# Values channel-major, a last inverse from 16x16 blocks, an early attention output and like tile addresses in a hybrid attention and RWKV-7 layer

## The chip, the cores and the metric

The kernel runs on one core of one Trainium2 chip. The time is the device time of one launch in microseconds (us); for the kernel before it is the median of three runs. A core has TensorE (PE, matrix products; PEld is its weight load), VectorE (DVE), ScalarE (ACT), GpSimd (POOL) and SyncE (SP, whose queue starts the transfers). Each engine works through its own list of instructions in order.

## The reference

One layer of a decoder over 512 positions of width 1024, all in 32-bit floats. What matters here:

```python
ada = (c @ w_ada + b_ada)                      # six rows of 1024: shift, scale and gate, twice
h = rms_norm(x, norm1_w) * (1.0 + sc1) + sh1
att_in, rwkv_in, gate_in = split(h @ w_in)
# attention: 3 groups of (window, dilation), 8 heads of 64 channels, blocks of 128 queries
p = exp(scores - m); den = sum(p)
num = einsum('bnrhqk,bnkrhe->bnqrhe', p, v)    # "values"
out_g = num / den_g; lse_g = m_g + log(den_g)
y_att = sum_g(softmax_g(lse)[..., None] * out_g) @ w_att_out     # "shares" of the groups
# RWKV-7: 16 heads, a 64x64 state each, one step a position
state = state * w_t + (state @ a_t) b_t + v_t k_t
y_rwkv = (group_norm(state @ r_t) + bonus) * g @ w_rwkv_out
x = x + gt1 * ((sigmoid(g_att) * y_att + sigmoid(g_rwkv) * y_rwkv) @ w_o)
x = x + gt2 * (silu(conv(gate)) * conv(val)) @ w_down            # after adaLN(x) @ w_up
out = rms_norm(x, norm_f_w)
```

## The kernel before

Products with weights are made of three products of a high and a low half (`mm`, L148: high by high, high by low, low by high), each 128x128 stationary and 512 columns moving. A weight comes as `raw` by DMA, ACT copies its high half `whi` (L193, L1136) and DVE subtracts the low half `wlo` (L194, L1139). Products of attention and of the recurrence are single 32-bit products. Transposes go through PE with `ident` (`tr`, L151).

**Order.** Up to the end of the recurrence the work is a list of tasks with an engine, a guessed cost in us, the tasks that they need, a priority and the buffers that they take and give (`Plan.add`, `Plan.run`, L47). The plan is run once at build time with those costs, and the order in which tasks start there is the order of the instructions on each engine. What comes after (`rwkv_out`, the mixing with `w_o`, the feed-forward part) is in the order of the code, as the tile scheduler lays it out. PE's order mixes long rows of 512-column products, used as filler, with the short steps that wait for other engines.

**Attention.** Three groups `gi`. For a block `n` of 128 queries and a pair of heads `i`, `scores` (`sc`) go through DVE (`sm`) and ACT (`pr`, exponentials) to PE transposes (`pt`), are copied to `pts`, and `values` gives `po`: here the probabilities `pts` are stationary (128x128) and `v` moves (64 columns), so a row is a query. `out` copies `po` to `o`. Groups 0 and 1 are later combined with the shares (`al` tasks): DVE multiplies `o` by the share (L1017), PE transposes the result (`pa<-ident,o`), ACT copies it to `attT` and a DMA stores it to `att_d`.

**Conditioning.** `w_ada` comes in 512 KB pieces `araw` through two buffers; DVE adds them into `acc` (L347), PE sums `acc` over partitions (`ada`).

**Recurrence.** Eight pairs of heads in four groups `g`; each group has a preparation (`pair`), an `inverse` and a `chain`. The sequence is cut into eight chunks of 64. The inverse of unit triangular 64x64 matrices is made of 32x32 blocks: DVE steps on all blocks at once, two columns a step (L1512, L1514, L1515) and then single ones (L1504, L1505), transposes (L1521, L1526), and two PE rounds `pe` of 32 products each that join the blocks (copies at L1567 and L1569). The chain then goes chunk by chunk: `xy` (state by inputs), `xs` (L1641), solve into `u`, `uv` (L1654), output `xo`, state `mbd` (L1664) with `mp` from POOL (L1646). It starts with a fill of `u` (L1589) and the product `u<-cen,v`.

**Gates and outputs.** Sixteen gate rows of 128 channels (`pg` tasks, `early_gate`) are made as filler, stored to `gate_d` and loaded back (L1825, `early_gates`) once the preparation's buffers are closed (`t0`); `t1` comes after group 0 and 2's tiles are closed too. `att_out` loads `att_d` (L1841), splits it (`ahi` L1843, `alo` L1844) and forms `pa` with `w_att_out`; `pr` is the same for the recurrence with `y`. Then `o` (with `w_o`, weights `wohi`, `wolo`), `u` (w_up, moving `h2hi`, `h2lo`) and `o` again (w_down).

Of the kernel before, what the change touches and what calls it, by code (L numbers as in the profile page):

```python
# [128 lines left out]
class Layer:  # L129
# [72 lines left out]
    def consts(self):  # L202
        nc, ctx, tc = self.nc, self.ctx, self.tc
        self.cp = cp = ctx.enter_context(tc.tile_pool(name="cp", bufs=1))
        self.dr = ctx.enter_context(tc.tile_pool(name="dr", bufs=1, space=DRAM))
        self.ident = cp.tile([P, P], F32, name="ident")
        make_identity(nc, self.ident)
        self.ones = cp.tile([P, 1], F32, name="ones")
        nc.gpsimd.memset(self.ones, 1.0)
        self.mhalf = cp.tile([P, 1], F32, name="mhalf")  # L210
# [9 lines left out]
        self.sel2 = cp.tile([P, 2], F32, name="sel2")  # L220
# [411 lines left out]

    def mask2(self):
# [38 lines left out]
    def attention(self):  # L672
# [4 lines left out]
        o = [ap.tile([P, 4, ATT_W], F32, name="o0"), None]  # L677
# [110 lines left out]
        def attend(gi, hf, order, blocks, width, mask, V, ready, prio):  # L788
# [4 lines left out]
            for n, i, new, end in order:  # L793
# [37 lines left out]
                def values(n=n, i=i, d=d, new=new, end=end):  # L831
                    if new:
                        pos[n] = self.aps.tile([P, 256], F32, tag="po", name=self.n("po"), bufs=2)
                    vs = V(n)
                    for h in range(2):
                        cs = slice(i * P + h * 64, i * P + h * 64 + 64)
                        for j, v in enumerate(vs):
                            self.mm(pos[n][:, cs], d["pts"][:, h, j * P : (j + 1) * P], v[:, cs],
                                    new and h == 0 and j == 0, end and h == 1 and j == len(vs) - 1)

                def out(n=n, i=i, new=new):
                    c0, c1 = (i * P if new else 0), i * P + P
                    if gi and o[1] is None:
                        o[1] = ap.tile([P, 4, ATT_W], F32, tag="o1", name="o1")
                    nc.scalar.copy(o[gi][:, n, hf * 256 + c0 : hf * 256 + c1], pos[n][:, c0:c1])
# [11 lines left out]
                t = pe(0.9 * wd / 256, values, [t], S0, take=("po",) if new else (), give=("pts",), name="po")  # L857
# [110 lines left out]
        for _ in ada:  # L968
            pass

# [23 lines left out]
        scaled = []  # L994
        for gi in range(2):
            a, b = stt[gi], oth[gi]
            mn, ea, eb, dn = [ap.tile([P, 4, 8], F32, name=f"{s}{gi}") for s in ("mn", "ea", "eb", "dn")]

            def diff(a=a, b=b, mn=mn, ea=ea, eb=eb):
                nc.vector.tensor_tensor(mn, a[:, :, 0, :], b[:, :, 0, :], op=ALU.min)  # L1000
                nc.vector.tensor_tensor(ea, mn, a[:, :, 0, :], op=ALU.subtract)
                nc.vector.tensor_tensor(eb, mn, b[:, :, 0, :], op=ALU.subtract)

            def exps(ea=ea, eb=eb):
                nc.scalar.activation(ea, ea, AF.Exp)
                nc.scalar.activation(eb, eb, AF.Exp)
# [12 lines left out]
            t = sca(0.45, exps, [t], name="al")  # L1019
            t = dve(1.2, share, [t], name="al")  # L1020
            scaled += [dve(0.7, lambda n=n, scale=scale: scale(n), [t, *outs[gi]], name="al") for n in range(4)]
        for i in range(4):
            d = {}

            def turn(i=i, d=d):
                d["pa"] = self.aps.tile([P, S], F32, tag="pt", name=self.n("pa"), bufs=2)
                for n in range(4):
                    self.tr(d["pa"][:, n * P : (n + 1) * P], o[0][:, n, i * P : (i + 1) * P], n == 0, False)
                for n in range(4):
                    self.tr(d["pa"][:, n::4], o[1][:, n, i * P : (i + 1) * P], False, n == 3)  # L1030

            def out(d=d):
                d["t"] = self.awl.tile([P, S], F32, tag="attT", name=self.n("attT"), bufs=2)
                nc.scalar.copy(d["t"], d["pa"])
            t = pe(0.95, turn, scaled, take=("pt",), name="pa")
            t = sca(0.6, out, [t], take=("attT",), give=("pt",), name="pa")
# [4 lines left out]
    def rwkv(self, tail):  # L1041
# [17 lines left out]
        def half():  # L1059

            self.half = self.ip.tile([P, 2], F32, name="half")
            nc.vector.tensor_reduce(self.half, self.ident.rearrange("p (q s y) -> p s q y", q=4, s=2), axis=AX.XY,
                                    op=ALU.add)
# [7 lines left out]
        for g in range(4):  # L1071
            for i in range(2):
                self.pair(g, i)
            self.inverse(g)
            self.chain(g)
        for m in range(2 * KD):
            self.early_gate(m)
# [12 lines left out]
        self.att_out(t1)  # L1090
# [480 lines left out]

    def chain(self, g):
# [42 lines left out]
        for c in range(NCH):  # L1615
# [62 lines left out]
            so_ = pe(0.33 if c else 0.0, state_out, [st], C_ + 0.01, take=("xo",), name="xo")  # L1678
# [26 lines left out]
        for i in range(2):  # L1705
# [43 lines left out]
            t = pe(1.05, gate, [t, self.sgs], S_, take=("t",), give=("g2",), name="gg")  # L1749
            gt_ = sca(0.6, gate_out, [t], E_, take=("gg",), give=("t",))  # L1750
# [32 lines left out]
    def norm(self, yts, t, deps, T_):  # L1783
# [9 lines left out]
        def var():  # L1793
            d["var"] = cw.tile([P, 4], F32, tag="var", name=self.n("var"))
            nc.vector.tensor_reduce(d["var"], d["sq"], axis=AX.X, op=ALU.add)

        def scale():
            rs = cw.tile([P, 4], F32, tag="rs", name=self.n("rs"))
# [19 lines left out]
    def gates(self, opened):  # L1818
# [4 lines left out]
        def load(m):  # L1823
            self.p[m] = self.pp2.tile([P, S], F32, name=f"gate{m}", tag=f"gate{m}")
            nc.sync.dma_start(self.p[m], self.gd[m])  # L1825
        for m in range(KD):
            self.pt[m] = self.pl.add("DMA", 0.8, lambda m=m: load(m), [opened, self.gdt[m]], M_, lag=2.0, name="gate in")

    def early_gates(self, pool):
        self.tr_ = [pool.tile([P, S], F32, name=f"gate{m}", tag=f"gate{m}") for m in range(KD, 2 * KD)]  # L1830
# [16 lines left out]
    def open_late(self, pool, lp):  # L1847

        self.lp = lp
        self.ahi, self.alo = [pool.tile([P, 4, S], F32R, name=x, tag=x) for x in ("ahi", "alo")]  # L1850
        self.yhi, self.ylo = [lp.tile([P, KD, S], F32R, name=x, tag=x) for x in ("yhi", "ylo")]

    def att_out(self, opened):

        nc = self.nc
        parts = [self.load_part(lambda k=k: self.att_d[:, k, :], lambda k=k: self.ahi[:, k, :],
                                lambda k=k: self.alo[:, k, :], lambda: self.lp, [opened], 0.01 * k) for k in range(4)]
        for m in range(KD):
            t, d = self.body("pa", self.w_att_out[0][:, m * P : (m + 1) * P], 4, "psb", lambda: self.psb("pa"),
                             lambda k: (self.ahi[:, k, :], self.alo[:, k, :]), deps=[opened], late=parts)  # L1860
# [181 lines left out]
    def ffn_down(self, xp, op, psx):  # L2042
# [30 lines left out]
        for n in range(NT):  # L2073
# [4 lines left out]
            ss, sofar = op.tile([P, 3], F32, name=self.n("ss"), tag="ss2"), None  # L2078
# [36 lines left out]
def hybrid_layer_kernel(ctx, tc, out, *args, dbg=None):  # L2115
# [11 lines left out]
    with ExitStack() as mix:  # L2127
# [7 lines left out]
        def tail():  # L2135
            L.psb = psum(att, "bps", 2, side="right")
            L.pp2 = right.enter_context(pool("pp2", side="right"))

            def more():
                yp = right.enter_context(pool("yp", side="right"))  # L2140
                L.open_late(att.enter_context(pool("attp", side="right")), yp)
            return more
# [3 lines left out]
        L.early_gates(right.enter_context(pool("gtp", side="right")))  # L2146
# [58 lines left out]
```

## Time and profile before

| | |
|---|---|
| Runs | 1233.17, 1234.45, 1236.06 us; median 1234.45 |
| Profiled execution | 1231.72 us, span 1230.0 us, mean granted clock 0.984 |
| PE busy | 1179.3 us, 96% of the span |
| DVE, ACT, POOL busy | 750.2, 542.4, 109.2 us |
| Moved by DMA | 139.41 MB, mean 113 GB/s |

A row of the timeline has the start, the duration, the engine, the line of the kernel, the operation, out<-in, the array shape (rows*columns of the PE array in use), partitions x elements, and a count; in brackets stands the idle time ahead of it and what ended it. Products overlap, so the pace is read from one start to the next, not from the durations. A row of the windows has the stretch, its length, the busy time of each engine with the count of its instructions, the clock that TensorE was granted, the share of DMA time and GB/s. One matmul of a 32-bit product shows twice in the trace (x8 for four).

### The profile page before, as it was taken

The page shows a single profiled execution, that of the slowest core. Times are in us where ns is not written, and L with a number is a line of the kernel's source. Part 1 is how long each engine was busy: PE and PEld are TensorE (multiplying, and loading weights), DVE is VectorE, ACT ScalarE, POOL GpSimd, SP SyncE. Part 2 cuts the span into 40 slices and gives each one's busy share as a digit, 9 for nine tenths or more (in the row PEclk, how much of TensorE's full clock was granted, in tenths as well). Part 3 has the DMA queues.
Part 4 walks back from the last instruction along what each step waited for, and adds up shares of the span by engine and source line. Part 5 has one row for each costly group of instructions (what it writes and reads, how often), then busy time and mean ns, then how long its engine had stood idle before and what let it go on. Part 6 is the DMA issues. An engine that isn't in the chain of part 4 may idle for free.

```text
span 1230.0 us, 18481 instructions
## 1 busy us (share of the span) xinstructions
PE 1179.3 (96%) x7200; PEld 946.1 (77%) x7200; DVE 750.2 (61%) x1266; ACT 542.4 (44%) x1011; POOL 109.2 (9%) x228
## 2 busy tenths in 40 slices
PE   4999999999999999999999599999999999999997
PEld 3788887889778776767786467788888888878886
DVE  5687862431668977846896844764556556652135
ACT  4374521522565474465545443444444444442123
POOL 4000000000000013132103122014000000000001
PEclk9899999999999999999999799999999999999999
DMA  9845872120233342413241525460232323233331
GB/s 316 249 132 166 273 229 66 45 80 18 69 103 94 90 112 74 126 47 98 80 114 43 163 58 178 156 206 18 69 103 86 103 86 102 86 103 103 103 120 68
DMA packets 168902, 139.41 MB, mean 113 GB/s; under 512 B 8849, under 2 KB 150251, under 8 KB 168815
## 3 DMA queue, kind: packets, MB, share of 16 engines
q1 hardware_dynamic: 168671, 137.98, 37.0%
q8 instruction: 56, 0.92, 0.3%
q14 instruction: 31, 0.25, 0.1%
q10 hardware_dynamic: 144, 0.26, 0.1%
HBM read 127.65 MB, written 10.56 MB: 112 GB/s over the span
## 4 chain that ended last, share of the span: by engine, by line
PE 79%; DVE 11%; DMA 6%; ACT 2%; issue 2%; SPq 0%; POOL 0%; POOLq 0%; DVEq 0%; ACTq 0%
PE u L148 22%; PE o L148 13%; PE v L148 7%; PE pg L148 7%; PE qk L148 5%; DMA araw<-in_w_ada_dram 4%; PE k L148 3%; PE r L148 2%; PE pa L148 2%; PE pr L148 2%; PE early L148 2%; PE po L148 2%; PE xy L148 2%; PE pt L151 1%; DVE tt L1514 1%
## 5 line engine op out<-in xcount | busy, mean ns | idle before, releaser
L194 DVE TENSOR_TENSOR wlo<-raw,whi 128x1024 fp32r<-128x1024 f32 x65 | 79.7, 1225 | 146.7 <-ACT whi L193 146.6
L148 PE MATMUL u<-h2lo,whi 128*128 128x512 f32 (+2 forms) x368 | 142.3, 387 | 0.0
L148 PE MATMUL u<-h2hi,whi 128*128 128x512 f32 (+2 forms) x368 | 142.3, 387 | 0.0
L148 PE MATMUL u<-h2hi,wlo 128*128 128x512 f32 (+2 forms) x368 | 142.2, 386 | 0.0
L1136 ACT CAST whi<-raw 128x1024 fp32r<-128x1024 f32 (+2 forms) x73 | 72.5, 994 | 123.7 <-PE qk L148 49.5
L193 ACT CAST whi<-raw 128x1024 fp32r<-128x1024 f32 x65 | 68.2, 1049 | 106.5 <-PE o L148 53.7
L1139 DVE TENSOR_TENSOR wlo<-raw,whi 128x1024 fp32r<-128x1024 f32 (+2 forms) x73 | 83.7, 1149 | 19.1 <-ACT whi L1136 18.8
L148 PEld LDWEIGHTS u<-h2lo,whi 128*128 128x128 f32 x368 | 68.9, 187 | 16.0 <-POOL h2lo L405 0.2
L148 PEld LDWEIGHTS u<-h2hi,wlo 128*128 128x128 f32 x368 | 68.9, 187 | 15.5
L148 PEld LDWEIGHTS u<-h2hi,whi 128*128 128x128 f32 x368 | 68.9, 187 | 15.4
L2028 DVE SCALAR_TENSOR_TENSOR u<-u,cols,u 128x511 f32<-128x511 f32 x88 | 65.7, 747 | 4.3 <-ACT u L2026 2.7
L148 PE MATMUL qk<-hhi,wlo 128*128 128x512 f32 x160 | 64.0, 400 | 0.0
L148 PE MATMUL qk<-hlo,whi 128*128 128x512 f32 x160 | 63.6, 397 | 0.0
L148 PE MATMUL qk<-hhi,whi 128*128 128x512 f32 x160 | 63.5, 397 | 0.0
L148 PE MATMUL o<-whi,fhi 128*128 128x512 f32 x144 | 56.1, 390 | 0.3 <-DVE u L2028 0.3
L148 PE MATMUL o<-wlo,fhi 128*128 128x512 f32 x144 | 56.0, 389 | 0.0
L148 PE MATMUL o<-whi,flo 128*128 128x512 f32 x144 | 56.0, 389 | 0.0
L148 PE MATMUL pg<-hhi,wlo 128*128 128x512 f32 x128 | 51.8, 405 | 0.0
L148 PE MATMUL pg<-hlo,whi 128*128 128x512 f32 x128 | 51.7, 404 | 0.0
L148 PE MATMUL pg<-hhi,whi 128*128 128x512 f32 x128 | 51.7, 404 | 0.0
L810 DVE CUSTOM_DVE_ANT_0 sm<-sc,m 128x256 f32<-128x256 f32 (+1 forms) x64 | 23.9, 404 | 37.6 <-PE sc L148 36.5
L347 DVE SCALAR_TENSOR_TENSOR acc<-araw,cols,acc 128x1024 f32<-128x1024 f32 x28 | 35.8, 1280 | 17.2 <-DMA araw<-in_w_ada_dram 17.1
(414 smaller groups left out, 2778.3 us busy)
## 6 DMA issues: line engine op xcount, KB each, us to landing
raw<-in_w_in_dram SPq DMA_DIRECT2D x62, 512.0 KB
raw<-in_w_up_dram SPq DMA_DIRECT2D x44, 512.0 KB
araw<-in_w_ada_dram SPq DMA_DIRECT2D x32, 512.0 KB
raw<-in_w_down_dram SPq DMA_DIRECT2D x22, 512.0 KB
araw<-in_w_ada_dram SPq DMA_DIRECT2D x32, 256.0 KB
wvraw<-in_w_in_dram SPq DMA_DIRECT2D x20, 256.0 KB
gate_d<-gs SPq DMA_DIRECT2D x16, 256.0 KB
gate<-gate_d SPq DMA_DIRECT2D x16, 256.0 KB
```

Of the source, the lines that this page charges most:

```text
L148: return self.nc.tensor.matmul(out, lhsT, rhs, start=start, stop=stop)
L151: self.nc.tensor.matmul(out, in_, self.ident[: in_.shape[0], : in_.shape[0]], is_transpose=True, start=start, stop=stop,)
L193: self.nc.scalar.copy(hl[0], raw)
L194: (lo_eng or self.nc.vector).tensor_tensor(hl[1], raw, hl[0], op=ALU.subtract)
L347: nc.vector.scalar_tensor_tensor(d["acc"], raw, ck, d["acc"], op0=ALU.mult, op1=ALU.add)
L810: nc.vector.tensor_tensor_reduce(d["sm", h][:, :wd], d["sc"][h][:, :wd], m[:, 256 - wd : 256] if gi == 0 else m[:, :wd], 1.0, 3.0e38, op0= ...
L1136: nc.scalar.copy(d["w"][0], d["raw"])
L1139: nc.vector.tensor_tensor(d["w"][1], d["raw"], d["w"][0], op=ALU.subtract)
L1514: nc.vector.tensor_reduce(t[:, n0:, j - 1 : j + 1], x, axis=AX.X, op=ALU.add)
L2028: nc.vector.scalar_tensor_tensor(u[:, d:], pu[:, : S - d], ch(c), u[:, d:], op0=ALU.mult, op1=ALU.add)
```

## The change

1. `values` has `v` stationary (128x64, one head) and the probabilities moving (128 columns); the two heads of a pair go to the two halves of `po`'s partitions. A row of `po` and `o` is now a channel.
2. The groups' shares are no longer multiplied into `o` ahead of the transposes. The shares (8 heads by 128 queries, four times) are transposed, split into halves in `share`, and spread over the channels by a product with a selector, `pw<-share,heads`; DVE multiplies `o` by `pw` from PSUM and POOL adds the two groups into `attT`. `heads` is filled on POOL.
3. Group 3's inverse is `inverse16`: blocks of 16x16, so six pair steps and three single ones, and two more PE rounds (`half_pe`, 64 products of 32x16 each) ahead of the two old ones; `first` is a fill and a copy on POOL.
4. Gate 7 is made after `t0` straight into its place, with no store or load.
5. `att_out` opens at `t0` instead of `t1` and loads `att_d` in two pieces of 512 KB through the weights' `raw` buffers; its halves `ahi`, `alo` are eight tiles that share room with gates 8 to 15.
6. In a chunk's `state` the products with `uv` come ahead of those with `mbd`, and `state_out` has the priority to follow at once.
7. Small tiles are packed (`ones`, `mhalf`, `sel2`, `half` in `few`; `var` and `rs` in one tile; `sup` narrower), so that the tiles behind them begin at other addresses.

```diff
-        self.ones = cp.tile([P, 1], F32, name="ones")
+        few = cp.tile([P, 8], F32, name="few")
+        self.ones, self.mhalf, self.sel2, self.half = few[:, 0:1], few[:, 1:2], few[:, 2:4], few[:, 4:6]
...
-                    for h in range(2):
-                        cs = slice(i * P + h * 64, i * P + h * 64 + 64)
-                        for j, v in enumerate(vs):
-                            self.mm(pos[n][:, cs], d["pts"][:, h, j * P : (j + 1) * P], v[:, cs],
+                    for j, v in enumerate(vs):
+                        for h in range(2):
+                            c0 = i * P + h * 64
+                            self.mm(pos[n][h * 64 : h * 64 + 64, i * P : i * P + P], v[:, c0 : c0 + 64],
+                                    d["pts"][:, h, j * P : (j + 1) * P], new and j == 0, end and j == len(vs) - 1)
...
-            def scale(n, gi=gi, ea=ea):
-                ov = o[gi][:, n, :].rearrange("p (h e) -> p h e", h=8)
-                nc.vector.tensor_tensor(ov, ov, ea[:, n, :].unsqueeze(2).to_broadcast([P, 8, 64]), op=ALU.mult)
+            def turn(gi=gi, d=d):
+                d["ps"] = self.aps.tile([P, S], F32, tag="pt", name=self.n("pe"), bufs=2)
+                for n in range(4):
+                    self.tr(d["ps"][:8, n * P : (n + 1) * P], shares[gi][1][:, n, :], n == 0, n == 3)
...
+                self.mm(d["w", gi], self.heads[:, i * P : (i + 1) * P], self.share[gi], True, True)
+            def scale(gi, i=i, d=d):
+                nc.vector.tensor_tensor(o[gi][:, i, :], o[gi][:, i, :], d["w", gi], op=ALU.mult)
-                nc.scalar.copy(d["t"], d["pa"])
+                nc.gpsimd.tensor_tensor(d["t"], o[0][:, i, :], o[1][:, i, :].rearrange("p (r j) -> p j r", r=4), op=ALU.add)
...
-            self.inverse(g)
+            (self.inverse16 if g in (3,) else self.inverse)(g)
             self.chain(g)
+        self.late = range(7, KD)
...
-        self.att_out(t1)
+        self.att_out(t0)
...
+        for j in range(14, 2, -2):
+            t = dve(0.55 + 2 * (16 - j) ** 2 / 480, lambda j=j: two(j), [t], name=f"inv{g}")
+        for j in range(2, -1, -1):
+            t = dve(0.37 + (16 - j) ** 2 / 480, lambda j=j: step(j), [t], name=f"inv{g}")
+        t = [dve(0.27, wide0, [t], E_), sca(0.42, wide1, [t], E_)]
+        tc = dve(1.1, rows, t, E_)
+        t = dve(0.72, rows11, [tc], E_)
+        for j in range(2):
+            t = pl.add("PE", 2.6, lambda j=j: half_pe(j), [t, ey], 0.5, take=() if j else ("t",), name="pe")
+            tc = t = sca(0.42, lambda j=j: half_out(j), [t], 0.5, name="pe")
+        t11 = dve(0.72, rows11, [tc], 0.5)
...
+                for i, h, cs, ci in ih:
+                    self.mm(xy[X[i], cs], gt(i, h, R[i], X[i]), s["uv"][R[i], ci], h == 0, c == 0 and h == 1)
                 for i in range(2 if c else 0):
-                    self.mm(xy[X[i], :P], prs[i]["ar"][:, c, X[i]], mbd(i), True, False)
-                for i, h, cs, ci in ih:
-                    self.mm(xy[X[i], cs], gt(i, h, R[i], X[i]), s["uv"][R[i], ci], c == 0 and h == 0, h == 1)
+                    self.mm(xy[X[i], :P], prs[i]["ar"][:, c, X[i]], mbd(i), False, True)
...
+            if m in self.late:
+                t, d = self.body("gate", self.gate_w(m), KD, "mm", lambda: self.mmp("pg"), self.hT)
+                self.pt[m] = self.pl.add("ACT", 0.7, lambda m=m, d=d: here(m, d), [t, opened], E_, give=("mm",))
...
+            d["t"] = self.wp.tile([P, D], F32, tag="raw", name=self.n("raw"), bufs=2).rearrange("p (k s) -> p k s", k=2)
+            nc.sync.dma_start(d["t"], self.att_d[:, 2 * q : 2 * q + 2, :])
```

The order of instructions at three places. First PE around a unit of values in group 0, in the kernel before (`qk` is the projection for the next queries and keys, used as filler):

```order
L148 MATMUL qk_1656<-hlo,whi_1582 128x512
L148 MATMUL qk_1656<-hhi,wlo_1583 128x512
L148 MATMUL po_1667<-v_1263,pts_1654 128x64 x4
L148 MATMUL qk_1656<-hhi,whi_1582 128x512
L148 MATMUL qk_1656<-hlo,whi_1582 128x512
```

and in the changed kernel:

```order
L148 MATMUL qk_1515<-hhi,whi_1416 128x512
L148 MATMUL qk_1515<-hlo,whi_1416 128x512
L148 MATMUL po_1652<-pts_1642,v_1276 64x128 x4
L148 MATMUL qk_1515<-hhi,wlo_1417 128x512
L148 MATMUL qk_1661<-hhi,whi_1508 128x512
L148 MATMUL qk_1661<-hlo,whi_1508 128x512
```

The unit has the same count of products, with the operands swapped, and it still stands between 512-column products. Second, PE at the end of group 2's chain, before (`t` are group 2's output transposes, `pe` the two rounds that end group 3's inverse, `u_6943` opens group 3's chain):

```order
L151 MATMUL t_6824<-ident,yt_6603 128x128
L151 MATMUL t_6824<-ident,yt_6734 128x128
L151 MATMUL t_6840<-ident,yt_6317 128x128
L151 MATMUL t_6840<-ident,yt_6472 128x128
L151 MATMUL t_6840<-ident,yt_6603 128x128
L151 MATMUL t_6840<-ident,yt_6734 128x128
L148 MATMUL pe_6856<-lt_6496,gt_5851 32x32 x32
L148 MATMUL pe_6856<-tt_6527,lt_6496 32x32 x32
L148 MATMUL u_6943<-cen,v_5833 64x128
```

and in the changed kernel, from the last product of chunk 5 to chunk 6's solve (`pe_6720` with 32x16 are the half rounds):

```order
L148 MATMUL xo_6684<-uv_6583,gt_5222 64x64 x4
L148 MATMUL pe_6720<-lr_6416,gt_5881 32x16 x64
L148 MATMUL xy_6803<-uv_6715,gt_5222 64x64 x4
L148 MATMUL xy_6803<-mbd_84,ar_4931 64x128
L148 MATMUL xy_6803<-mbd_85,ar_5554 64x128
L148 MATMUL xo_6816<-mbd_84,ar_4931 64x128
L148 MATMUL xo_6816<-mbd_85,ar_5554 64x128
L148 MATMUL pe_6720<-lt_6417,lr_6416 32x16 x64
L148 MATMUL u_6246<-xs_6886,gt_5222 64x64 x4
L148 MATMUL pa_6896<-a_6564,whi_6791 128x512
L148 MATMUL pa_6896<-a_6568,whi_6791 128x512
L148 MATMUL pa_6896<-a_6564,wlo_6792 128x512
```

The half rounds stand inside group 2's chain, the first between `xo` of one chunk and `xy` of the next, and the `pa` products come in there; before, the rounds stood behind the whole chain. Third, DVE in group 3's inverse, before (the last pair steps and the first single one; `mbd` is group 2's state):

```order
L1664 SCALAR_TENSOR_TENSOR mbd_86<-u_6232,pc_4931,mp_6686 128x128
L1664 SCALAR_TENSOR_TENSOR mbd_87<-u_6232,pc_5483,mp_6686 128x128
L1512 TENSOR_TENSOR tt_6527<-tt_6527,lt_6496 128x676
L1514 TENSOR_REDUCE tt_6527<-tt_6527 128x13x2
L1515 SCALAR_TENSOR_TENSOR tt_6527<-tt_6527,sup_6537 128x13
L1512 TENSOR_TENSOR tt_6527<-tt_6527,lt_6496 128x784
L1514 TENSOR_REDUCE tt_6527<-tt_6527 128x14x2
L1515 SCALAR_TENSOR_TENSOR tt_6527<-tt_6527,sup_6537 128x14
L1504 TENSOR_TENSOR tt_6527<-tt_6527,lt_6496 128x450
L1505 TENSOR_REDUCE tt_6527<-tt_6527 128x15
```

and in the changed kernel (the last pair step and the single ones; `a_6568` is a low half of the attention input):

```order
L1689 TENSOR_TENSOR lr_6416<-lt_6417 128x288
L1691 TENSOR_REDUCE lt_6417<-lr_6416 128x12x2
L1692 SCALAR_TENSOR_TENSOR lt_6417<-lt_6417,sup_6500 128x12
L2003 TENSOR_REDUCE var_6612<-sq_6600 128x4
L1682 TENSOR_TENSOR lr_6416<-lt_6417 128x182
L1683 TENSOR_REDUCE lt_6417<-lr_6416 128x13
L1682 TENSOR_TENSOR lr_6416<-lt_6417 128x210
L1683 TENSOR_REDUCE lt_6417<-lr_6416 128x14
L2085 TENSOR_TENSOR a_6568<-raw_6572,a_6564 128x512
L1682 TENSOR_TENSOR lr_6416<-lt_6417 128x240
L1683 TENSOR_REDUCE lt_6417<-lr_6416 128x15
L1870 SCALAR_TENSOR_TENSOR mbd_84<-u_6246,pc_4847,mp_6595 128x128
```

Steps are shorter and fewer between two states of the chain, and the splits of `att_out` now stand among them.

More of the change, by code (lines that the diff above doesn't have):

```diff
@@ L631, in masks, with share_rows @@
                 pattern=[[-1, P]], channel_multiplier=1)
+    def share_rows(self):
+        nc = self.nc
+        self.heads = self.awl.tile([P, 2, S], F32R, tag="qk12", name="heads", bufs=1)[:40, 0, :]
+        t = self.awl.tile([P, 2, S], F32R, tag="qk02", name="share", bufs=1)[:40]
+        self.share = [t[:, gi, :] for gi in range(2)]
+        one = lambda r, c: self.ident[r, c : c + 8].unsqueeze(2).to_broadcast([r.stop - r.start, 8, 64])
+        h = self.heads.rearrange("p (h e) -> p h e", e=64)
+        for r, c in ((slice(0, 32), 0), (slice(32, 40), 32)):
+            nc.gpsimd.tensor_copy(h[r], one(r, c))
+        for x in self.share:
+            nc.gpsimd.tensor_copy(x[:32].rearrange("p (h e) -> p h e", e=64), one(slice(0, 32), 64))
     def mask2(self):
@@ L856, in attend @@
                 t = (dve if i else sca)(0.68 if wd == 256 else 0.42, turned, [t], E0, take=("pts",), give=("pt",), name="pts")
-                t = pe(0.9 * wd / 256, values, [t], S0, take=("po",) if new else (), give=("pts",), name="po")
+                t = pe(0.1 + 0.45 * wd / 256, values, [t], S0, take=("po",) if new else (), give=("pts",), name="po")
                 last[i].append(t)
@@ L969, in attention @@
             pass
+        heads = pl.add("POOL", 3.0, self.share_rows, sc, E_, take=("qk02", "qk12"), name="heads")
         def pre():
@@ L1037, in attention @@
+            t = pl.add("POOL", 1.2, out, ts, E_, take=("attT",), name="pa")
             pl.add("DMA", 0.8, lambda i=i, d=d: nc.sync.dma_start(self.att_d[:, i, :], d["t"]), [t], W_, lag=2.0,
@@ L1073, in rwkv @@
                 self.pair(g, i)
[L1074 removed]
+            (self.inverse16 if g in (3,) else self.inverse)(g)
             self.chain(g)
+        self.late = range(7, KD)
         for m in range(2 * KD):
[L1077 removed]
+            if m not in self.late:
+                self.early_gate(m)
         def close_pre():
```

223 lines of the change are left out of this document (184 added, 39 removed).

## The prediction

> **What bounds the kernel now.** I read the page's busy times first, then the span cut into stretches, then the timeline inside each stretch where TensorE (PE) is not full.
>
> ```profile
> span 1230.0 us, 18481 instructions
> PE 1179.3 (96%) x7200; PEld 946.1 (77%) x7200; DVE 750.2 (61%) x1266; ACT 542.4 (44%) x1011; POOL 109.2 (9%) x228
> 180.00:190.00 10.00, 7.31 (x28) 4.92 (x27) 8.02 (x8) 1.06 (x1) 1.06 (x4) 0.87 0.69 208
> 680.00:690.00 10.00, 7.14 (x93) 4.90 (x88) 8.68 (x20) 3.94 (x12) 3.52 (x5) 0.96 0.46 151
> 690.00:700.00 10.00, 2.90 (x15) 1.72 (x13) 9.64 (x18) 5.36 (x10) 2.17 (x3) 0.50 0.64 193
> 700.00:710.00 10.00, 5.54 (x138) 4.88 (x139) 7.81 (x13) 4.82 (x10) 0.00 (x0) 0.50 0.53 144
> 720.00:757.00 37.00, 37.00 (x361) 24.78 (x358) 14.22 (x29) 15.05 (x44) 9.71 (x20) 1.00 0.23 69
> ```
>
> PE is the bound nearly everywhere: of 51 us without PE work, the stretches from 680 to 710 hold 2.86 + 7.10 + 4.46 = 14.4 us, and 180 to 190 holds 2.7; most of the rest lies at the start. From 690 to 710 the granted clock is 0.50. Elsewhere a saving counts only if it takes time out of PE's own queue. The gap at 690 ends on VectorE (DVE):
>
> ```profile
> 664.56 2.04 DVE L1473 STREAM_TRANSPOSE lt<-ld 128x1024 f32<-128x1024 f32 x1 [0.20 <-ACT ld L1469]
> 670.83 0.17 DVE L1512 TENSOR_TENSOR tt<-tt,lt 128x4 f32<-128x4 f32 x1
> 690.42 0.97 DVE L1514 TENSOR_REDUCE tt<-tt 128x28 f32<-128x784 f32 x1
> L1512 DVE TENSOR_TENSOR tt<-tt,lt 128x4 f32<-128x4 f32 (+13 forms) x14 | 6.4, 458 | 0.3
> L1515 DVE SCALAR_TENSOR_TENSOR tt<-tt,sup 128x1 f32<-128x1 f32 (+13 forms) x14 | 3.6, 258 | 0.5
> L1512 DVE TENSOR_TENSOR tt<-tt,lt 128x196 f32<-128x196 f32 x1 | 0.4, 363 | 0.0
> 675.94 0.44 PE L148 MATMUL xy<-mbd,ar 128*64 128x128 f32 x4
> 682.10 0.44 PE L148 MATMUL xy<-mbd,ar 128*64 128x128 f32 x4
> 695.79 0.48 PE L151 MATMUL t<-ident,yt 128*128 128x128 f32 x1 [4.45 <-POOL yt L1801]
> 700.03 1.92 PE L148 MATMUL pe<-lt,gt 32*32 32x32 f32 x64 [1.06 <-DVE y L1765]
> 708.29 1.12 PE L148 MATMUL u<-cen,v 128*64 128x128 f32 x8 [3.03 <-DVE u L1589]
> ```
>
> Group 3's inverse begins its steps at 670.8 and is still in them at 690.4, when group 2's chain has run out (one of its last transposes `t` waits 4.45 us for POOL). Group 3's chain starts at 708.29. A chunk of the chain takes 682.10 - 675.94 = 6.2 us.
>
> **Values, channel-major: -2.3 us.** There are 28 full units of four matmuls of 64 columns (x8 in the trace) and four half ones. Their like in the new shape is the `u<-cen,v` group.
>
> ```profile
> 158.20 0.39 PE L148 MATMUL qk<-hlo,whi 128*128 128x512 f32 x1
> 158.43 1.00 PE L148 MATMUL po<-v,pts 128*128 128x64 f32 x8
> 159.24 0.48 PE L148 MATMUL qk<-hhi,wlo 128*128 128x512 f32 x1
> 159.55 0.39 PE L148 MATMUL qk<-hhi,whi 128*128 128x512 f32 x1
> 443.82 0.39 PE L148 MATMUL pg<-hhi,wlo 128*128 128x512 f32 x1
> 444.14 0.66 PE L148 MATMUL u<-cen,v 128*64 128x128 f32 x8
> 444.73 0.50 PE L148 MATMUL pg<-hhi,whi 128*128 128x512 f32 x1
> 445.07 0.40 PE L148 MATMUL pg<-hlo,whi 128*128 128x512 f32 x1
> 528.11 0.61 PE L148 MATMUL u<-cen,v 128*64 128x128 f32 x8
> 528.55 0.40 PE L148 MATMUL xo<-uv,gt 128*64 128x64 f32 x8
> ```
>
> Between groups of its own array shape (128*64) the new form takes 528.55 - 528.11 = 0.44 us against 159.24 - 158.43 = 0.81. But in the new order nearly every unit stands alone between 128*128 work. There I count from the matmul ahead to the second one behind, less two plain ones of 0.23: old 159.55 - 158.20 - 0.46 = 0.89, new 445.07 - 443.82 - 0.46 = 0.79. So 0.10 a unit, 28 units, -2.8; a half unit goes from about 0.45 to 0.79 - 4 x 0.05 = 0.58, four of them, +0.5. The bounds are 0 and 28 x (0.89 - 0.44) = 12.6; I take the lone row since the neighbours are the same kind. The Trainium skill's TensorEngine Tiling (Array Packing), Performance Considerations, recommends just this swap for a free size of 64 and gives 2x; 28 x 0.4 = 11 us would follow. The same page's Key Properties say that "Changing tiling mode (not just tile) drains the TensorE", and the lone row agrees: 0.32 instead of 0.23 on the way in, 0.59 instead of 0.44 inside.
>
> **State's shares in one go: 0.** It removes 32 transposes, eight DVE scalings and four ACT copies, and adds eight transposes, eight 512-column products over 40 rows, eight DVE scalings, two DVE splits and four POOL adds.
>
> ```profile
> L151 PE MATMUL pa<-ident,o x32: 270/273/330, 330.2 to 334.0; 128*128 128x128 f32 x32
> 187.86 1.87 PE L148 MATMUL ada<-acc,ones 128*1 128x256 f32 x4 [2.69 <-DVE acc L347]
> ```
>
> Removed: 3.9 us. Added: 8 x 0.12 + 8 x 0.23 = 2.8, or 4.4 with 0.2 of shape change at each product. Between -1.1 and +0.5; with two or three us of longer chain in front of the next stage, hidden by the k, r and v projections that the new order places between, I take 0.
>
> **The conditioning row: -3.3 us.** The row above shows PE waiting 2.69 us for the last `acc`, then four short matmuls in 1.87. The new order puts 36 more `v` matmuls (36 x 0.23 = 8.3 us) in front, so PE arrives after `acc` is there. Gone are the 2.7 and some 0.6 at low clock (0.87 in that stretch). Bounds: 0, if the last load slides as well, and 3.7.
>
> **Group 3's inverse from 16x16 blocks: -9.3 us with the gap.** Nine steps replace seventeen. A DVE product of 196 elements takes 363 ns, one of 4 takes 170: 0.17 us and 1.0 ns per element. The nine products of the new order have 1360 elements in all, so 9 x 0.17 + 1.4 = 2.9 us; as much again for their reductions, and 6 x 0.26 for the corrections at L1515: 7.4 us. The old fourteen pair steps alone took 2 x 6.4 + 3.6 = 16.4. The blocks' transpose (2.04) halves too. Added are two half rounds on PE, 64 products of 32x16 each, with a copy after each and a second transpose. The order puts the first round between chunks 5 and 6 of group 2; by the rows its input is ready some 3.5 us after chunk 5 begins, about 680, and group 3's chain can start about 691 instead of 708.3. What can be won is the 14.4 us of idle time and the half clock:
>
> ```profile
> 637.70 1.20 PE L148 MATMUL pe<-lt,gt 32*32 32x32 f32 x64 [0.19 <-DVE lt L1526]
> 638.83 0.50 PE L148 MATMUL pg<-hhi,whi 128*128 128x512 f32 x1
> 709.34 0.80 PE L148 MATMUL pa<-ahi,whi 128*128 128x512 f32 x1
> 709.94 0.63 PE L148 MATMUL pa<-alo,whi 128*128 128x512 f32 x1
> ```
>
> The 64-entry round takes 1.92 at 700 and 1.20 at 637.7, twice; `u<-cen` 1.12 for 0.66; `pa` 0.60 apart instead of 0.23 for the first few: together 4 us, so 18.4. Against it: two rounds of 128 entries at 1.13 / 64 = 18 ns, plus 0.3 for the changes of shape: 5.1 us. An entry of 16 columns was not seen; half the time and the same time bound it at 2.8 and 5.1, and I take the same. The Trainium skill's TensorEngine Tiling (Array Packing), Instruction Overhead, gives 60 cycles whatever the size up to 60 columns, 256 x 25 ns = 6.4 us as an estimate, 1.9 more than the 4.5 of the rows. Of the idle time some 4 us stays: around chunks 5 and 6 the new order has no filler between products but the rounds themselves, and each must wait for a DVE or ACT step of 0.3 to 0.7 us. 18.4 - 5.1 - 4.0 = 9.3. Bounds: -15 with no remainder, -3 with one chunk (6.2) of it more.
>
> **Attention output opened earlier, one late gate: +1 us.** The late gate's 24 matmuls are the same, moved behind the closing of the preparation; one store and one load of 256 KB go. The `pa` products fill the old gap, so fewer are left for group 3's chain, where PE was full (37.00 of 37.00). The new order still has 8 to 14 of them a chunk, then `pr`. DVE gets four `alo` splits ahead of chunk 6's state; the loads are issued about 20 us earlier, since the last early gate ends before chunk 3, and cover that. At the end the old order had single `o` products as filler while the last `ylo` came; the new one goes straight through `pr`. I put +1 there, between 0 and 3.
>
> **Tiles alike modulo 256: -7.5 us.**
>
> ```profile
> 900.00:1000.00 100.00, 100.00 (x430) 80.17 (x429) 39.35 (x54) 25.20 (x36) 1.00 0.32 93
> 1110.00:1210.00 100.00, 100.00 (x443) 82.84 (x442) 2.08 (x3) 0.00 (x0) 1.00 0.29 95
> 851.31 0.34 PE L148 MATMUL u<-h2hi,whi 128*128 128x384 f32 x1
> 854.49 0.34 PE L148 MATMUL u<-h2hi,whi 128*128 128x384 f32 x1
> 858.31 0.34 PE L148 MATMUL u<-h2lo,whi 128*128 128x384 f32 x1
> 861.08 0.34 PE L148 MATMUL u<-h2hi,wlo 128*128 128x384 f32 x1
> ```
>
> The first row is of `u` alone, the second of `o`: the same shape runs at 100/430 = 233 ns in `u` and 226 in `o`, both at full clock. As built, `h2` stands at 224 modulo 256 and the weights of `u` at 32, while `o` has like residues. Inside `u` the two kinds meet: from 851.31 to 854.49 (weights at 32) 18 starts take 3.18 us, 177 ns each; from 858.31 to 861.08 (weights at 224) 16 take 2.77, 173 ns. After the change both sides are alike everywhere: 1008 wide `u` products x 6.5 ns = 6.5 us, and about 1 us in `pr` and `pa`. Bounds 0 and 8: the other reading of these rows is DVE's and ACT's traffic, 39 and 25 us of a hundred in `u` against 2 and 0.
>
> **Sum.** -2.3 + 0 - 3.3 - 9.3 + 1 - 7.5 = -21.4, so a span of 1208.6 us from 1230.0. The profiled execution took 1231.72, 2.7 under the median of 1234.45 (1233.17 to 1236.06); against that median, 1213.
>
> **Rivals.**
> Alignment is worth nothing, and `u` is slow through its neighbours' traffic: 1213 + 7.5 = 1220.
> The gap closes by half: a half round that is a chunk late holds chunks 6 and 7 behind it in PE's queue, since PE runs in order: +6, 1219.
> The values take their stream time, 0.44 a unit, because the drain hides behind the weights' load: -10, 1203. The lone rows speak against it.
> Slower than before: the inverse's half rounds block PE. Everything of group 2 behind the first one waits with it, one us for one us. It decides when the round becomes ready 22 us after 680, at 702, as late as the old round at 700. For it: `first` now sits on POOL between behind a group scaling like the one that made PE wait 4.45 us in the old gap; against it: five such waits would be needed. From 1237.
> No change: PE's gap merely moves to chain 3, whose filler `pa` was, and alignment is nothing: 1233.
>
> **How the numbers follow.** My case 0.52, with 1207 to 1218 of its own; alignment nothing 0.15; gap half closed 0.14; values at stream speed 0.11; slower 0.04; no change 0.04. A measurement here can tell 0.2%, 2.5 us. 1202 to 1222 leaves out the last two and part of the pairs of rivals together. Faster 0.92, same 0.04, slower 0.04.
>
> **What would show it.** Values: `po` groups of 128*64 standing 0.59 apart between 128*128 work, not 0.44. Gap: group 3's `u<-cen` near 690, with the clock at 1.00 up to then. Conditioning: `ada` without a wait on `acc`. Alignment: 440 or more `u` products in 100 us instead of 430. I am wrong if PE's idle time after 670 is above 8 us, or if `u` keeps 233 ns.

## The result and the profile after

The changed kernel took 1215.46 us in the median of four runs (1214.15 to 1222.0) beside 1233.81 before: a ratio of 0.987, 95% interval 0.9836 to 0.9904. Beside the second set of experiments it took 1219.26, ratio 0.9905 (0.9877 to 0.9934). The forecast was 1213, range 1202 to 1222. So it is faster by 1 to 1.3%, on the slow side of the forecast and inside the range.

The profile shown is the run of 1222.0 us. Its mean granted clock is 0.984; the three others of the first four have 0.990 or 0.991 and 1214 to 1216 us. First the head of the page, then stretches of the span (busy time of PE, PEld, DVE, ACT and POOL, then the granted clock), the last row for `u` alone.

```profile
span 1220.3 us, 18960 instructions
PE 1175.0 (96%) x7440; PEld 935.6 (77%) x7440; DVE 741.8 (61%) x1250; ACT 542.4 (44%) x1012; POOL 113.0 (9%) x236
...
180.00:190.00 10.00, 10.00 (x45) 9.77 (x44) 6.02 (x5) 1.64 (x2) 0.00 (x0) 1.00 0.83 258
500.00:520.00 20.00, 16.50 (x193) 13.10 (x192) 16.73 (x26) 9.02 (x13) 0.00 (x0) 0.99 0.30 99
560.00:580.00 20.00, 18.45 (x131) 14.03 (x130) 12.09 (x23) 6.03 (x13) 3.78 (x7) 1.00 0.38 104
680.00:700.00 20.00, 17.57 (x459) 13.43 (x459) 10.21 (x20) 10.89 (x28) 5.35 (x8) 0.75 0.36 112
700.00:720.00 20.00, 20.00 (x211) 14.27 (x210) 10.13 (x21) 8.72 (x24) 2.56 (x5) 0.82 0.29 86
780.00:800.00 20.00, 16.53 (x68) 11.88 (x67) 14.24 (x17) 8.16 (x10) 0.00 (x0) 1.00 0.53 163
900.00:1000.00 100.00, 100.00 (x443) 82.84 (x442) 40.68 (x56) 25.85 (x37) 1.00 0.35 100
```

The old gap is closed: from 680 to 710 PE lacked 14.4 us, from 680 to 720 it now lacks 2.4. `u` runs 443 products in 100 us instead of 430, with DVE and ACT as busy as before. But these stretches show three new losses: 3.5 us at 500 to 520, 1.55 at 560 to 580, 3.5 at 780 to 800. The timeline shows the places:

```profile
79.65 0.39 PE L148 MATMUL qk<-hhi,whi 128*128 128x512 f32 x1
79.97 0.66 PE L148 MATMUL po<-pts,v 128*64 128x128 f32 x8
80.56 0.51 PE L148 MATMUL qk<-hlo,whi 128*128 128x512 f32 x1
165.48 1.95 PE L148 MATMUL ada<-few,acc 128*128 128x1 f32 x16 [0.92 <-DVE acc L347]
191.79 1.02 PE L148 MATMUL ada<-acc,few 128*1 128x256 f32 x4 [0.53 <-DVE acc L347]
335.20 0.79 PE L148 MATMUL r<-hhi,whi 128*128 128x512 f32 x1 [1.26 <-DVE lt L1187]
519.33 1.04 PE L148 MATMUL u<-cen,v 128*64 128x128 f32 x8 [1.86 <-DVE u L1795]
683.30 0.45 PE L148 MATMUL u<-xs,gt 64*64 64x64 f32 x8 [0.23 <-ACT xs L1847]
685.43 1.26 PE L148 MATMUL pe<-lr,gt 32*32 32x16 f32 x128
686.62 0.56 PE L148 MATMUL xy<-uv,gt 64*64 64x64 f32 x8
688.22 0.73 PE L148 MATMUL pe<-lt,lr 32*32 32x16 f32 x67 [0.37 <-ACT lr L1727]
689.90 0.92 PE L148 MATMUL pe<-lt,lr 32*32 32x16 f32 x61 [0.95 <-issue]
708.01 0.66 PE L148 MATMUL u<-cen,v 128*64 128x128 f32 x8
782.60 0.50 PE L148 MATMUL pr<-yhi,whi 128*128 128x512 f32 x1 [1.88 <-ACT whi L193]
```

A unit of values takes 0.32 in and 80.56 - 79.97 = 0.59 inside. A half round of 128 entries takes 686.62 - 685.43 = 1.19 us. At 519.33 group 1's chain waits for the fill of `u` on DVE, behind that group's own inverse; at 708.01 group 3's chain starts; at 782.60 `pr` waits for a weight.

### The profile page after: what moved, and what is told of

It reads as the page before. It is cut to its first block, busy times and chain, and to the rows that moved or that the text cites. A ratio compares the mean times of both kernels' runs of the same rounds, so it can differ in the third digit from the quotient of the medians.

```text
span 1220.3 us, 18960 instructions
## 1 busy us (share of the span) xinstructions
PE 1175.0 (96%) x7440; PEld 935.6 (77%) x7440; DVE 741.8 (61%) x1250; ACT 542.4 (44%) x1012; POOL 113.0 (9%) x236
## 4 chain that ended last, share of the span: by engine, by line
PE 79%; DVE 10%; DMA 4%; ACT 3%; issue 2%; SPq 0%; POOL 0%; POOLq 0%; DVEq 0%; ACTq 0%
PE u L148 22%; PE o L148 13%; PE qk L148 8%; PE v L148 7%; PE pg L148 6%; PE k L148 3%; PE r L148 3%; PE pa L148 2%; PE xy L148 2%; PE pt L151 2%; DMA raw<-in_w_rwkv_out_dram 2%; PE sc L148 1%; PE early L148 1%; PE po L148 1%; DVE wlo L1177 1%
```

## The experiments

Ratios are to the kernel before, run on the same chip in the same set. The first four rows are the first set, the next four the second and the last four the third.

| Run | Parts in it | Median us | Ratio, 95% interval |
|---|---|---|---|
| b_align | only `u`'s addresses | 1225.02 | 0.9956 (0.9938 to 0.9973) |
| a_shift | all, `u` unlike again | 1224.6 | 0.9953 (0.9930 to 0.9975) |
| a_inv32 | all but the new inverse | 1240.24 | 1.0074 (1.0056 to 1.0092) |
| a_oldval | all but values and shares | 1215.05 | 0.9858 (0.9830 to 0.9887) |
| after_again | all | 1219.26 | 0.9905 (0.9877 to 0.9934) |
| a_pw128 | all, shares with 128 rows | 1220.41 | 0.9912 (0.9888 to 0.9935) |
| a_oldstate | all but the state order | 1222.4 | 0.9925 (0.9899 to 0.9951) |
| b_inv16 | new inverse and addresses | 1218.63 | 0.9890 (0.9860 to 0.9921) |
| a_oldval_again | as a_oldval | 1212.64 | 0.9838 (0.9818 to 0.9859) |
| a_att_t1 | all but early output, late gate | 1220.43 | 0.9891 (0.9872 to 0.9911) |
| b_inv16_state | inverse, addresses, state order | 1229.09 | 0.9966 (0.9950 to 0.9983) |
| a_oldval_state | inverse, addresses, early output, late gate | 1211.24 | 0.9817 (0.9793 to 0.9841) |

**Addresses (b_align, a_shift).** One unused tile behind `h2lo`, 48 floats in the kernel before and 16 in the changed one:

```diff
         self.h2lo = hp2.tile([P, KD, S], F32R, name="h2lo", tag="h2lo")
+        hp2.tile([P, 48], F32, name="shift", tag="shift")
```

> The kernel before with one unused 192-byte tile behind h2lo, so that h2 starts at 32 modulo 256 like the weights of u; nothing else is moved. If the addresses make u slow: u at 226 to 227 ns instead of 233, 1008 x 6.5 ns, so 6.5 us faster than before (ratio 0.9947) and about 440 products in 100 us. If the traffic of DVE and ACT makes it slow: no change (ratio 1.000).

> The changed kernel with one unused 64-byte tile behind h2lo, so that h2 starts at 160 modulo 256 and the weights of u at 224. If unlike residues cost time whatever their distance: u back at 233 ns and 6.5 us slower than the changed kernel (about 1222, ratio to before 0.990 to 0.992). If only the old distance did it, or if addresses are nothing: as the changed kernel, 1215 (ratio 0.985 to 0.987).

Windows of `u`, first b_align, then a_shift:

```profile
900.00:1000.00 100.00, 100.00 (x443) 82.81 (x442) 40.84 (x57) 25.24 (x36) 1.00 0.33 96
```

```profile
900.00:1000.00 100.00, 100.00 (x430) 80.13 (x429) 38.53 (x54) 25.23 (x36) 1.00 0.33 95
```

An unused tile alone turns 430 into 443, with the traffic of DVE and ACT unchanged, and another turns 443 back into 430. So the addresses are the cause, and the traffic is not. All 1008 wide `u` products together take 235.3 us in the kernel before and in a_shift, 228.6 in b_align and in the changed kernel: 6.7 us in both pairs. Only one distance was tried, though: from the weights to `h2` it was 224 - 32 = 192 before, and in a_shift 160 - 224 = -64, which is 192 again modulo 256. b_align is worth 0.44%, 5.4 us (interval 3.3 to 7.6), where 6.5 was expected. a_shift has 1224.6 where the changed kernel had 1215.5 and 1219.3; across sets that agrees with 6.5 but can't measure it, and its ratio of 0.9953 lies above the 0.990 to 0.992 that was expected.

**The inverse (a_inv32, b_inv16).** In a_inv32 `self.inverse(g)` stands for all groups. b_inv16 is the kernel before with `inverse16` for group 3 and the packed tiles.

```diff
-            (self.inverse16 if g in (3,) else self.inverse)(g)
+            self.inverse(g)
```

> The changed kernel with the old inverse of 32x32 blocks for group 3 too. If the 16x16 blocks close the gap, as forecast: 9 us slower than the changed kernel (about 1224, ratio 0.993), PE idle for some 12 us around group 3's start. If the profiled 7.4 us of half clock behind the half rounds eats the gain in most runs: within 3 us of it (1213 to 1218).

> The kernel before with two parts alone: group 3's inverse from 16x16 blocks, and the packed small tiles (like residues). Attention output still opens at t1, after group 2's chain, so the first three chunks of group 3's chain have no pa products as filler. By my sum: -7.5 for the tiles and -9.3 for the gap, 1215. If the inverse pays only with attention output opened early: the gap is cut by less than half, and the time is 1220 to 1226.

a_inv32 is not 9 but some 21 to 25 us slower than the changed kernel, and slower than the kernel before. Its windows at group 3's chain, and then those of b_inv16 at the old gap:

```profile
720.00:740.00 20.00, 16.14 (x228) 12.04 (x228) 9.46 (x16) 7.56 (x19) 1.83 (x2) 0.83 0.40 120
740.00:760.00 20.00, 17.39 (x206) 12.29 (x206) 3.85 (x12) 7.93 (x26) 6.55 (x14) 0.88 0.13 40
760.00:780.00 20.00, 12.61 (x104) 9.31 (x102) 6.27 (x14) 5.55 (x16) 4.37 (x8) 0.50 0.00 0
```

```profile
680.00:700.00 20.00, 15.49 (x487) 12.10 (x486) 5.27 (x11) 10.59 (x29) 4.35 (x8) 0.79 0.57 180
700.00:720.00 20.00, 19.57 (x185) 13.83 (x183) 13.25 (x28) 11.87 (x31) 5.72 (x9) 0.79 0.44 124
```

With the old inverse and the early output the `pa` filler is spent before group 3's chain (all 96 products start between 688 and 716), which then starves for 60 us (13.9 us idle from 720 to 780, clock down to 0.50). So in this kernel the early output needs the short inverse. The short inverse does not need the early output: b_inv16 leaves 4.9 us idle from 680 to 720 where 14.4 stood, and took 1218.6, between its two forecasts of 1215 and 1220 to 1226. Against b_align's 0.9956 that is 8 us for the inverse with the `pr` and `pa` addresses; the two sets' intervals leave 2 to 14.

**Values, shares and state order (the other eight).** a_oldval puts back the values with queries as rows, DVE's scaling and the transposes. a_pw128 widens the selector and the shares with zeros (the loops that fill the new rows are left out here):

```diff
-        self.heads = self.awl.tile([P, 2, S], F32R, tag="qk12", name="heads", bufs=1)[:40, 0, :]
-        t = self.awl.tile([P, 2, S], F32R, tag="qk02", name="share", bufs=1)[:40]
+        self.heads = self.awl.tile([P, 2, S], F32R, tag="qk12", name="heads", bufs=1)[:, 0, :]
+        t = self.awl.tile([P, 2, S], F32R, tag="qk02", name="share", bufs=1)
...
```

a_oldstate puts back the order `mbd` before `uv` and the old priority of `state_out` (cost 0.33, `C_ + 0.01`). a_oldval_state is a_oldval with the same, b_inv16_state is b_inv16 with the new order, and a_att_t1 has `self.att_out(t1)` and all gates early.

> The changed kernel with the old values (queries as rows), the old scaling of o and the old 32 transposes. By my forecast of these two parts (values -2.3, shares 0): 2.3 us slower than the changed kernel, 1217.7. By the reading of the trace after, where each of the eight products of the shares stands alone with 40 rows (0.63 instead of 0.23 us) and a 1.26 us wait and half a clock follow: shares cost 4 to 5 us, so 2 us faster, about 1213. If the values were worth their stream time: 8 us slower.

> The changed kernel once more, on the chip of the three others of this call, so that they can be set against it. Expected 1214 to 1222: in the first four runs three stood near 1215 with a mean granted clock of 0.991 and one at 1222 with 0.984, the profiled one, where the clock is at 0.51 from 690 to 700.

> The changed kernel with the selector and the shares filled with zeros up to 128 rows, so that the eight products pw have 128 rows instead of 40 and the array keeps its shape between them and the filler. If the change of shape is what made them dear (0.63 us each instead of 0.23 in the trace after): 8 x 0.4 = 3.2 us faster, and DVE's scalings come sooner. If the wait between scalings sets the pace: no change.

> The changed kernel with a chunk's state products in the old order (mbd ahead of uv) and the old priority of state_out. In the trace after PE loses 3.5 us of idle time and some at low clock where group 1's chain starts (510 to 530), which the kernel before does not; as built, the order with the old state has 12 k products between the rounds of that inverse there instead of four. If that is the cause: the stall goes, 4 to 5 us faster than the changed kernel. If the new state order saves elsewhere what it loses there: the same, or 2 us slower.

> The changed kernel with the old values and shares once more, beside the three others of this call. Ratio to before 0.986 as the first time. Theory A (the shares lose 4 to 5 us, the values win 2): 0.986, 3 us under the changed kernel's mean of 0.9887. Theory B (everything beside the inverse and the tiles is worth nothing and the clock's dip decides): 0.989 like the others.

> The changed kernel without the early attention output and without the late gate (att_out at t1, four loads of its own, all sixteen gates early). Against the changed kernel this is what these two parts bring. Theory A: they bring the 4 us that the shares lose, so without them 0.992. Theory B: 0.989.

> The kernel before with the 16x16 inverse, the packed tiles and the new order of the state's products (uv first, state_out at once). Theory A, by the stall at group 1's start that vanished when the old state order was put back in the changed kernel: 4 us slower than without the new state order (0.992). Theory B: 0.989. If the new order shortens a chunk: 0.986.

> The kernel before with the 16x16 inverse, the packed tiles, the early attention output and the late gate; old values, shares and state order. Theory A: the best of all, 0.985, as the stall at group 1's start and the shares' cost are both away. Theory B: 0.989. If the stall only moves to later chunks, as in the run with the old state order alone (1222.4 beside 1219.3): 0.988 or more.

The shares first, in the timeline after and then with 128 rows:

```profile
328.20 0.50 PE L148 MATMUL pw<-share,heads 40*128 40x512 f32 x1
329.29 0.49 PE L148 MATMUL pw<-share,heads 40*128 40x512 f32 x1
330.38 0.49 PE L148 MATMUL pw<-share,heads 40*128 40x512 f32 x1
```

```profile
329.66 0.39 PE L148 MATMUL pw<-share,heads 128*128 128x512 f32 x1
330.36 0.40 PE L148 MATMUL pw<-share,heads 128*128 128x512 f32 x1
336.06 0.50 PE L148 MATMUL r<-hhi,whi 128*128 128x512 f32 x1 [2.51 <-DVE lt L1188]
```

Two filler products stand between two `pw`. With the change of shape a round takes 1.09 us, without it 0.70, so the shape does cost 0.4 each. Yet a_pw128 is not faster (1220.41 beside 1219.26): PE only comes earlier to `r`, and waits 2.51 instead of 1.26 us for DVE, which has eight scalings of 0.69 us and the weights' splits in front of `lt`. My reading that the shape sets the pace fell; DVE does.

The state order is read from the stretches 500 to 520 and 560 to 580. The rows of a_oldstate, b_inv16_state and a_oldval_state, in this order:

```profile
500.00:520.00 20.00, 19.80 (x219) 15.24 (x218) 13.08 (x21) 8.91 (x17) 0.00 (x0) 1.00 0.43 129
...
560.00:580.00 20.00, 20.00 (x122) 16.00 (x120) 13.59 (x24) 6.67 (x12) 2.07 (x5) 1.00 0.39 119
...
760.00:780.00 20.00, 16.93 (x66) 13.42 (x65) 14.75 (x22) 6.92 (x9) 0.87 (x2) 0.83 0.23 76
780.00:800.00 20.00, 16.63 (x68) 11.96 (x68) 13.81 (x18) 8.90 (x10) 0.00 (x0) 1.00 0.50 161
```

```profile
500.00:520.00 20.00, 18.02 (x184) 14.49 (x183) 17.53 (x24) 7.79 (x12) 0.00 (x0) 0.84 0.38 115
...
560.00:580.00 20.00, 18.34 (x122) 13.03 (x121) 9.14 (x16) 8.06 (x16) 4.54 (x6) 1.00 0.28 83
...
700.00:720.00 20.00, 14.92 (x180) 11.12 (x180) 10.93 (x23) 11.77 (x30) 4.38 (x7) 0.59 0.73 223
```

```profile
500.00:520.00 20.00, 19.95 (x217) 15.63 (x217) 14.66 (x23) 8.52 (x16) 0.00 (x0) 1.00 0.36 112
560.00:580.00 20.00, 19.92 (x118) 15.34 (x117) 12.55 (x21) 8.31 (x16) 2.59 (x4) 1.00 0.29 88
680.00:700.00 20.00, 18.00 (x516) 13.18 (x512) 10.60 (x20) 12.94 (x31) 4.46 (x8) 1.00 0.56 174
...
780.00:800.00 20.00, 20.00 (x90) 16.56 (x89) 13.57 (x17) 8.04 (x10) 0.00 (x0) 1.00 0.51 161
```

Every kernel with the new state order has the two losses (2.0 to 3.5 us and 1.6 us), every kernel without it has neither: it is their cause. The edit moves the products and changes the priority of `state_out` at once, and no run separates the two. In b_inv16_state it also moves idle time to 700, and the kernel is 0.0076 slower than b_inv16 by the ratios, 9 us, more than any of its expectations. Taken out of the changed kernel alone it gives nothing (a_oldstate, 1222.4 beside 1219.3, intervals overlapping): PE is idle for 6.4 us from 760 to 800 instead of 3.5, as `pr` waits for `yhi` and for a weight. That the filler kept at 510 is missing there is my reading and was not tested. Taken out together with the values and shares it does pay: a_oldval_state has PE full at 500, 560 and 780 and 0.9817, 1.4 us by the medians under a_oldval_again in the same set (overlapping intervals). It is the fastest kernel that was run. The changed kernel was not in that set; against its ratios of the two others (0.987 and 0.9905) the difference is 6 to 11 us, with intervals that just touch in the first and are apart in the second.

a_oldval beats the changed kernel's pooled ratios (0.9848 against 0.9888 by the means of two sets each, about 5 us). That is what theory A of the last set said of the values and shares together. But what they are worth depends on the parts around them. a_att_t1 and b_inv16_state, in one set, differ in the values and shares (and in which task takes the buffer `gg`): there the new ones are 9 us faster (0.9891 against 0.9966, intervals apart). a_oldstate and a_oldval_state differ in the values and shares alone: there the new ones are some 13 us slower (0.9925 against 0.9817, intervals apart, across sets). The early output is alike: with the new values it brings nothing (a_att_t1, 0.9891, where theory A had 0.992), with the old ones it is, with the late gate, the whole step from b_inv16's 0.989 to 0.9817. So no part has a price of its own, and why the values win in one surrounding and lose in another is open.

## Why the prediction was right, and where not

- **Gap and inverse, -9.3:** the size held, about 8 by b_inv16 against b_align (2 to 14), and 2.4 us of idle time are left of 14.4 where I had kept 4. The path did not hold. Group 3's `u<-cen` was to stand near 690 with the clock at 1.00 up to there; it stands at 708.01, against 708.29 before, and the clock is 0.51 from 690 to 700. From 680 to 720 PE is filled with `pa` products (15.8 us busy) instead of an earlier chain. In b_inv16 the chain starts at 695.3 and in a_oldval_state at 697.6, both with the old state order.
- **The sizes inside the gap:** a half round takes 1.19 us, 9.3 ns an entry, the lower bound that I had not taken. By the 60 cycles of the Trainium skill's TensorEngine Tiling (Array Packing), Instruction Overhead, the estimate of the prediction would be 3.2 us a round; the trace does not agree. On the other side, PE stops for 0.95 us within the second round without waiting for an engine, a term that the forecast lacks.
- **Alignment, -7.5:** held for `u`: 443 in 100 us against the 440 named, 6.7 us over its 1008 products. The rival of traffic is out. The 1 us for `pr` and `pa` was not measured.
- **Values, -2.3:** the unit's size held to the row (0.59 inside, foretold as 0.59; that is also the median of the 16 units between 512-column products). The drain of the Trainium skill's TensorEngine Tiling (Array Packing), Key Properties, agrees with these rows; the 2x of its Performance Considerations for the swap does not.
- **Conditioning, -3.3:** mis-sized. At the row that I named 0.53 of 2.69 us is left, but PE now waits 0.92 us at 165.48 ahead of an earlier `ada`. So 1.3 us of idle time is gone, and the mean clock from 160 to 200 is 0.96 in both kernels. The gain hangs on the new values: from 165 to 200 the profiles with the old ones wait 1.8 to 3.2 us for `acc`, those with the new ones 0.2 to 1.5.
- **Shares, 0:** mis-sized. The last product of values starts 5.5 us earlier than before (318.1 for 323.6), the first `pn` behind the shares only 1.4 (343.2 for 344.6), with 71 filler products between them in both: 4 us lost, from 0.4 us for the shape at each product, then 1.26 of waiting for DVE and 3 us of half clock. In after_again the wait is the same but the clock stays at 1.00, and this stretch takes 23.5 us instead of 25.1. The filler that I named does not hide the wait, as `lt` stands behind the scalings in DVE's queue.
- **State order:** the step that was missing. I gave it no term; it costs 3.5 + 1.55 us of PE at two other groups' starts, through the plan, and not in a chunk.
- **End, +1:** mis-sized; 3.5 us idle at 780 to 800, where `pr` waits for its weight. In a_oldval and in a_att_t1 PE is full there.

In the order values, conditioning, shares, gap, state order, end, alignment: -2.3 - 1.3 + 4 - 8 + 5 + 3.5 - 6.7 = -5.8, against -9.7 between the two profiled spans; the rest lies within the interval of the -8. The four terms that went wrong, conditioning, shares, state order and end, come to +11 where the forecast had -2.3. The forecast of -21 came out as -13 to -18 by the medians of the two sets. So two large terms were right, and that the result still fell inside the range is partly luck, as the terms account for only 6 us of the gain.

A sum by stages also does not tell what taking a part out will bring. Values, conditioning and shares come to +0.4 in it, yet a_oldval, without the three, is 5 us faster: PE's idle time there is 2.0 instead of 3.5 us at 500 to 520, 1.0 instead of 2.4 at 680 to 720 and none at 780 to 800. Of the signs of being wrong the first came close: PE idles 7.0 us from 670 to 1200 (8 was the limit; 16.2 before), and some 7.7 more behind 1200 in both kernels.

## What to carry to other kernels

A cost taken from a group of like instructions holds only beside the same neighbours: count from the instruction ahead to the second one behind, where the array changes shape. Where a planner writes the order, a changed cost or priority is a change at every place in the program; compare the order around each stage's start, above all the filler between two dependent steps, and not only where the edit is. Before a clever part is kept, try the others without it: here the new inverse, the like addresses and the early output with the late gate were enough, and the rest, added to them, took time away.

## What the runs showed of the hardware

The addresses of two operands set a product's pace: with `h2` and the weights 192 apart modulo 256 a 512-column product of `u` takes 233 ns, with like residues 226 to 227, with all else unchanged. As only this distance was tried, a period of 128 would look the same.

In the profile after, the clock fell behind 1.26 us of idle time, less than I had thought: at 335 eight `r` products ran at half pace. In after_again, the same program, the same wait left the clock at 1.00. First the row after, then two of after_again:

```profile
330.00:340.00 10.00, 8.74 (x26) 5.50 (x26) 8.07 (x11) 4.20 (x6) 7.04 (x5) 0.83 0.39 129
```

```profile
330.00:340.00 10.00, 8.74 (x42) 6.89 (x41) 7.46 (x11) 5.84 (x8) 5.15 (x4) 1.00 0.52 166
332.62 0.50 PE L148 MATMUL r<-hhi,whi 128*128 128x512 f32 x1 [1.26 <-DVE lt L1187]
```

In a_pw128 2.51 us of idle time at this place left the clock at 1.00, too. The Trainium skill's TensorE: Matmul & The Clock Gate, Part 1, names at least one idle window of about 3.4 us that runs freely. That one and the same wait is followed by half the clock in one run and not in another agrees with a free-running window; that 1.26 us was enough does not agree with a whole window of idle time.

The dip at 690 makes much of the difference of 7 us between runs of one kernel (1215 at 0.991, 1222 at 0.984). The faster runs have no profile, but a_shift has the same PE instructions in the same order, and its profiled run (mean clock 0.989) has far less of that dip. First two rows after, then a_shift:

```profile
690.00:700.00 10.00, 9.76 (x178) 7.31 (x180) 2.62 (x5) 5.15 (x12) 0.61 (x1) 0.51 0.24 74
700.00:710.00 10.00, 10.00 (x107) 7.32 (x105) 2.67 (x5) 3.21 (x9) 1.82 (x3) 0.64 0.25 68
```

```profile
690.00:700.00 10.00, 10.00 (x197) 7.50 (x194) 3.65 (x8) 5.97 (x14) 0.00 (x0) 0.87 0.11 33
700.00:710.00 10.00, 10.00 (x90) 6.79 (x90) 6.35 (x15) 5.58 (x16) 2.56 (x5) 1.00 0.55 169
682.14 0.45 PE L148 MATMUL u<-xs,gt 64*64 64x64 f32 x8 [0.23 <-ACT xs L1847]
701.08 0.66 PE L148 MATMUL u<-cen,v 128*64 128x128 f32 x8
```

From this solve to group 3's start PE takes 708.01 - 683.30 = 24.7 us after and 701.08 - 682.14 = 18.9 in a_shift: the dip costs 5.8 us. That the runs at 1215 lack the same dip is likely, but was not seen.

The stop in the rounds of short products comes with the half rounds: one to three such stops of 0.6 to 2.6 us stand in them or soon behind them in every profile with the new inverse, and none in the three with the old one (before, b_align, a_inv32). Each of the 15 ends 1.3 to 1.6 us after a 16 KB packet of the queue q8, which the page lists as `instruction`. That PE waits there for its own instructions is likely by this, and no run tests it.
